# First projection of an encoder block: both modulation vectors of a quarter in one VectorE pass, and a written order for all engines

## The chip, the cores and the metric

The kernel runs on one NeuronCore of a Trainium2 chip. The metric is the device time of one execution in microseconds (us). Three runs of the kernel before took 1404.02 to 1405.08 us, median 1404.52.

## What is computed

One encoder layer over 1024 tokens of width 1024. The change touches its beginning, the modulated norm and part of the first projection:

```python
mod = jax.nn.silu(c) @ w_ada[l] + b_ada[l]
shift1, scale1, gate1, shift2, scale2, gate2 = jnp.split(mod, 6, axis=-1)

h = rms_norm(x, norm1_g[l]) * (1.0 + scale1[:, None, :]) + shift1[:, None, :]
z = h @ w_in[l]
```

`x` is 1024 x 1024, `w_ada` 1024 x 6144 and `w_in` 1024 x 2112, all float32. Two attention groups, an output projection and a mixture of experts follow; they are the same in both kernels.

## The kernel before

**Precision.** A projection is done in three matmuls per block (`mm3`, lines 68 to 71): rounded activation by rounded weight, rounded activation by the weight's remainder, remainder of the activation by the rounded weight. So a weight tile `wraw` becomes `whi` (ScalarE, line 134) and `wlo` (VectorE, line 135), and the activations become `hThi` and `hTlo`, transposed, in eight blocks of 128 rows of the width.

**First half of the first projection.** It gives 512 columns of `z` (576 to 1087) for the first four tiles of 128 tokens (`zs`, four accumulators in PSUM). The width is worked off in four quarters `i`, two blocks each. A quarter needs 256 entries of `shift1` and 256 of `scale1`, so 2 x 1 MB of `w_ada`, and 0.5 MB of `w_in`. Its steps:

1. The products: `w_ada` lies with 8 rows `k` of the width in each of 128 partitions, and `sc` holds SiLU(c) the same way. `adaacc` is the sum over `k` of row times `sc[k]`. For `shift1` (except in quarter 0, which uses TensorE, line 295) ScalarE scales the rows (line 148) and GpSimd adds them in three passes (lines 149 to 151); for `scale1` VectorE does one scaling and seven multiply-adds of 256 columns (lines 143 and 145).
2. The column sums: four matmuls of `adaacc` by ones (line 300) into `pab`.
3. VectorE: `b1` (shift), `t8`, and `a1` = (1 + scale) x gain (lines 302 to 304).
4. Per block (`flip_x`): four transposes of x tiles (line 187), `hThi` on ScalarE (line 272), the same once more unrounded as `hf` on VectorE (line 273), `hTlo` = `hf` - `hThi` (line 274).
5. 24 projection matmuls (lines 69 to 71).

The x tiles are normalised first by `norm_x` (lines 260 to 266): square with a sum, root, reciprocal, scaling.

**Second half.** The other four x tiles (`xs2`) are loaded and normalised at the end of quarter 3 (line 264 scales them on ScalarE) and go through the same blocks, with rope on the finished outputs (`rope_q`, lines 173 to 178) in between. The first matmul of this half is the one at 72.21 us in the profile. `sinb` is the sine table, scaled once (line 315).

**What sets the order.** Before, a scheduler places the instructions of this stage on the engines. The loads are issued by SP, one after the other; an issue waits for the issue eight before it to have landed, and for its buffer. The tiles `s4` (10 buffers of 512 KB) hold `w_ada`, the second x tiles and later temporaries.

```python
def split_w(tiles, src, ks, width):
    raw, hi, lo = (w[:, ks, :width] for w in tiles)
    Y.dma_start(raw, src)
    A.copy(hi, raw)
    V.tensor_sub(lo, raw, f32(hi))
```

`Y` is SP, `A` ScalarE, `V` VectorE, `G` GpSimd, `T` TensorE.

Of the kernel before, what the change touches and what calls it, by code (L numbers as in the profile page):

```python
# [9 lines left out]
F32 = mybir.dt.float32  # L10
# [10 lines left out]
D = 1024  # L21
# [30 lines left out]
def tile_hymba(  # L52
# [86 lines left out]
    def ada_sum(pool, w, eng):  # L139

        acc = pool.tile([128, 256], F32, name="adaacc", tag="adaacc")
        if eng is V:
            V.tensor_scalar(acc, w[0][:, 0], sc[:, 0:1], None, op0=ALU.mult)
            for k in range(1, 8):
                V.scalar_tensor_tensor(acc, w[k // 4][:, k % 4], sc[:, k:k + 1], acc, op0=ALU.mult, op1=ALU.add)
        else:
            for k in range(8):
                A.activation(w[k // 4][:, k % 4], w[k // 4][:, k % 4], AF.Copy, scale=sc[:, k:k + 1])
            G.tensor_add(w[0], w[0], w[1])
            G.tensor_add(w[0][:, 0:2], w[0][:, 0:2], w[0][:, 2:4])  # L150
            G.tensor_add(acc, w[0][:, 0], w[0][:, 1])
        return acc
# [73 lines left out]
    with tc.tile_pool(name="s1a", bufs=2, **RT) as sa, tc.tile_pool(name="s1r", bufs=1, **RT) as sr:  # L226
        cc = sr.tile([128, 8], F32, name="cc")
        Y.dma_start(cc, c[0].rearrange("(p k) -> p k", k=8))
        A.activation(sc, cc, AF.Silu)
        rows = sr.tile([72, 128], F32, name="rows")  # L230
# [37 lines left out]
        def flip_x(xs, j, half):  # L268
# [4 lines left out]
            V.tensor_scalar(hf, ptr, a1[:, j:j + 1], b1[:, j:j + 1], op0=ALU.mult, op1=ALU.add)  # L273
# [5 lines left out]
        adas = [ada_load(0), ada_load(4)]  # L279
        xs = [load_x(t) for t in range(4)]  # L280
        for xt in xs:
            norm_x(xt, False)
        xs2 = []
        t8 = sr.tile([128, 8], F32, name="t8")
        for i in range(4):
            qs = slice(2 * i, 2 * i + 2)
            if i:
                adas = [ada_load(i), ada_load(4 + i)]
            split_w(wq0[i // 2], wi[:, 2 * i:2 * i + 2, 576:1088], slice(2 * (i % 2), 2 * (i % 2) + 2), 512)
            pab = mps()  # L290
# [15 lines left out]
            for j in range(2 * i, 2 * i + 2):  # L306
                flip_x(xs, j, 0)
# [1325 lines left out]
```

## Time and profile before

| | |
|---|---|
| runs, median (lowest to highest) | 1404.52 us (1404.02 to 1405.08) |
| profiled execution, its own time | 1404.29 us |
| its span in the profile | 1402.5 us |
| TensorE busy over the span | 1304.8 us (93%) |
| VectorE busy | 1082.4 us (77%) |
| ScalarE busy | 771.9 us (55%) |
| GpSimd busy | 537.5 us (38%) |
| first half of the first projection, first matmul of it | 24.48 us from the span's start |
| second half, first matmul | 72.21 us |

PE is TensorE's matmul row, PEld its weight loads, DVE VectorE, ACT ScalarE, POOL GpSimd, SP the queue that issues loads. Times in the rows are from the span's start. A matmul's duration holds its way through the array, which the next one overlaps, so their pace is read from the distance of two starts. In rows of stretches the number before the DMA columns is the granted clock of TensorE as a share of 2.4 GHz.

### The profile page before, as it was taken

The numbers are of one execution on the slowest core, as the hardware profiler recorded it, in microseconds if no ns is written. First come the engines' busy times: TensorE is split into PE (matmuls) and PEld (weight loads), VectorE is DVE, ScalarE is ACT, GpSimd is POOL, SyncE is SP. The second block draws the span as 40 slices with busy tenths as digits, with TensorE's granted clock in tenths as the row PEclk, the third lists the DMA queues.
The fourth block names the chain that finished last, engine by engine and source line by source line (L and its number), as shares of the span: only waits on it lengthen the run. The fifth ranks groups of instructions, "written<-read, shape, count | busy, mean of one in ns | idle before, by whom it ended". The sixth has DMA issues, their size and how long they took to land. (4 is left out here: it accounts for less than half of the span.)

```text
span 1402.5 us, 18267 instructions
## 1 busy us (share of the span) xinstructions
PE 1304.8 (93%) x6343; PEld 1050.9 (75%) x6343; DVE 1082.4 (77%) x1610; ACT 771.9 (55%) x1194; POOL 537.5 (38%) x361
## 2 busy tenths in 40 slices
PE   5799999887999999989995999999999989999993
PEld 4578789765888888878884777777777767777762
DVE  5887646557788888874568798888888888888876
ACT  5531224346666766661224667766666756666653
POOL 2102100047666666650002244444444532544332
PEclk9899999998999999999995999999999999999995
DMA  9528963681344525238966999999989997999946
GB/s 330 163 91 265 309 234 123 182 306 53 87 139 113 172 84 192 71 132 291 342 229 256 357 367 361 356 380 372 324 318 329 354 342 286 363 375 356 380 153 246
DMA packets 123969, 357.06 MB, mean 255 GB/s; under 512 B 15781, under 2 KB 41474, under 8 KB 122338
## 3 DMA queue, kind: packets, MB, share of 16 engines
q1 hardware_dynamic: 79794, 200.11, 41.1%
q10 hardware_dynamic: 29376, 113.25, 21.2%
q0 software_dynamic: 14704, 42.51, 10.0%
q8 instruction: 51, 0.84, 0.2%
q14 instruction: 44, 0.36, 0.1%
HBM read 306.52 MB, written 57.69 MB: 260 GB/s over the span
## 5 line engine op out<-in xcount | busy, mean ns | idle before, releaser
L1176 DVE TENSOR_TENSOR ra<-rb,ra 128x1024 fp32r<-128x1024 f32 x249 | 290.5, 1220 | 51.5 <-ACT ra L1175 47.3
L1348 POOL DMA_INDIRECT x_d<-y,tg x32 | 223.4, 6983 | 124.0 <-DVE y L1418 108.5
L1175 ACT CAST ra<-rb 128x1024 fp32r<-128x1024 f32 x249 | 242.4, 1049 | 1.9 <-PE pg L70 1.3
L626 PE MATMUL s<-ra 128*128 128x512 f32 x448 | 130.8, 409 | 5.1 <-DVE stg L592 3.1
L1176 DVE TENSOR_TENSOR ra<-rx,ra 128x1024 fp32r<-128x1024 f32 x103 | 120.5, 1217 | 17.0 <-ACT ra L1175 14.6
L647 ACT ACTIVATE e<-s,mx 128x1024 f32<-128x1024 f32 x96 | 107.5, 1120 | 38.4 <-DVE mx L642 21.5
L642 DVE TENSOR_REDUCE mx<-s 128x1 f32<-128x1024 f32 x96 | 116.7, 1217 | 12.4 <-PE s L626 12.3
L69 PE MATMUL pz<-whi,hThi 128*128 128x512 f32 (+2 forms) x320 | 118.6, 371 | 5.1 <-ACT hThi L272 5.1
L70 PE MATMUL pz<-wlo,hThi 128*128 128x512 f32 (+2 forms) x320 | 116.5, 364 | 0.4 <-DVE wlo L135 0.4
L69 PE MATMUL pg<-ra,xT 128*128 128x512 f32 x256 | 114.9, 449 | 0.1
L953 POOL DMA_INDIRECT xb<-h_d,tg x31 | 31.0, 999 | 219.1 <-PE ptr L1354 198.7
L71 PE MATMUL pz<-whi,hTlo 128*128 128x512 f32 (+2 forms) x320 | 112.8, 360 | 0.1
L70 PE MATMUL pg<-ra,xT 128*128 128x512 f32 x256 | 102.3, 400 | 6.9 <-DVE ra L1176 6.9
L658 ACT CAST rb<-ptr 128x512 fp32r<-128x512 f32 x128 | 74.3, 588 | 59.8 <-PE ptr L654 59.1
L69 PE MATMUL pu<-ra,xT 128*128 128x512 f32 x256 | 104.1, 407 | 0.0
L71 PE MATMUL pg<-ra,xT 128*128 128x512 f32 x256 | 102.9, 402 | 1.1 <-DVE xT L1437 1.1
L1175 ACT CAST ra<-rx 128x1024 fp32r<-128x1024 f32 x103 | 101.2, 1048 | 2.3 <-DVE ra L1176 1.4
L70 PE MATMUL pu<-ra,xT 128*128 128x512 f32 x256 | 101.1, 395 | 0.1
L71 PE MATMUL pu<-ra,xT 128*128 128x512 f32 x256 | 101.2, 395 | 0.0
L626 PEld LDWEIGHTS s<-ra 128*128 128x128 f32 x448 | 81.6, 191 | 22.8 <-ACT e L647 4.2
L659 DVE TENSOR_TENSOR rb<-ptr,rb 128x512 fp32r<-128x512 f32 x128 | 86.3, 680 | 9.7 <-ACT rb L658 9.5
L654 PE MATMUL ptr<-ident,e 128*128 128x128 f32 x512 | 78.0, 275 | 9.0 <-POOL e L802 5.3
(365 smaller groups left out, 3020.9 us busy)
## 6 DMA issues: line engine op xcount, KB each, us to landing
rb<-in_w_expert_up_dram ACTq DMA_DIRECT2D x26, 1024.0 KB
rb<-in_w_expert_down_dram ACTq DMA_DIRECT2D x26, 1024.0 KB
rb<-in_w_expert_gate_dram ACTq DMA_DIRECT2D x24, 1024.0 KB
rb<-in_w_expert_gate_dram SPq DMA_DIRECT2D x20, 1024.0 KB
rb<-in_w_expert_down_dram SPq DMA_DIRECT2D x20, 1024.0 KB
rb<-in_w_expert_up_dram SPq DMA_DIRECT2D x19, 1024.0 KB
aw<-in_w_ada_dram SPq DMA_DIRECT2D x32, 512.0 KB
ra<-qk_d SPq DMA_DIRECT2D x48, 256.0 KB
```

The lines of the kernel that those rows point to most:

```text
L69: T.matmul(ps, ahi, bhi, start=first, stop=False)
L70: T.matmul(ps, ahi, blo, start=False, stop=False)
L71: T.matmul(ps, alo, bhi, start=False, stop=last)
L626: T.matmul(ps[:, ns], l, r[:, ns], start=i == 0, stop=i == len(parts) - 1)
L642: V.reduce_max(mx, ps, axis=AX.X, negate=True)
L647: A.activation(e, ps, AF.Exp, bias=nb, scale=1.0, accum_out=z)
L654: T.transpose(ptr[:, i * 128:(i + 1) * 128], e[:, (4 * b + i) * 128:(4 * b + i + 1) * 128], ident)
L658: A.copy(hi[:, :, q], src)
L659: return lambda: V.tensor_sub(lo[:, :, q], src, f32(hi[:, :, q]))
L1175: A.copy(hi, raw[:, 2 * half:2 * half + 2])
L1176: V.tensor_sub(lo, raw[:, 2 * half:2 * half + 2], f32(hi))
L1348: G.indirect_dma_start(out=x2_d, out_offset=bass.IndirectOffsetOnAxis(ap=si, axis=0), in_=y, in_offset=None, bounds_check=S - 1, oob_is_er ...
```

## The change

- `w_ada` is loaded so that the 256 columns of `shift1` and of `scale1` lie side by side, in eight loads of 256 KB per quarter where there were four of 512 KB. One scaling and seven multiply-adds of 512 columns on VectorE give both sums. ScalarE's and GpSimd's part in it is gone, and so is quarter 0's way over TensorE. `adaacc` has one buffer.
- The four x tiles are loaded ahead of `w_ada`, and `hf` is made on ScalarE in both halves.
- The stage is written inside `manual_schedule`, so each engine runs its instructions as they stand in the text; products for quarter `i + 1` are laid between the steps of quarter `i`. The second x tiles are normalised two in quarter 2 and two in quarter 3.
- Per block, the eight matmuls with `hThi` come first and the four with `hTlo` after them.
- A root of a constant (`sqt`) is added behind the SiLU in the text.

```diff
@@ -136,19 +136,15 @@
 
     wa = w_ada[0].rearrange("(p k) n -> p k n", k=8)
 
-    def ada_sum(pool, w, eng):
-
-        acc = pool.tile([128, 256], F32, name="adaacc", tag="adaacc")
-        if eng is V:
-            V.tensor_scalar(acc, w[0][:, 0], sc[:, 0:1], None, op0=ALU.mult)
-            for k in range(1, 8):
-                V.scalar_tensor_tensor(acc, w[k // 4][:, k % 4], sc[:, k:k + 1], acc, op0=ALU.mult, op1=ALU.add)
-        else:
-            for k in range(8):
-                A.activation(w[k // 4][:, k % 4], w[k // 4][:, k % 4], AF.Copy, scale=sc[:, k:k + 1])
-            G.tensor_add(w[0], w[0], w[1])
-            G.tensor_add(w[0][:, 0:2], w[0][:, 0:2], w[0][:, 2:4])
-            G.tensor_add(acc, w[0][:, 0], w[0][:, 1])
+    def ada_sum(pool, w):
+
+        acc = pool.tile([128, 512], F32, name="adaacc", tag="adaacc", bufs=1)
+        for k in range(8):
+            wk = w[k // 2][:, k % 2].rearrange("p v n -> p (v n)")
+            if k == 0:
+                V.tensor_scalar(acc, wk, sc[:, 0:1], None, op0=ALU.mult)
+            else:
+                V.scalar_tensor_tensor(acc, wk, sc[:, k:k + 1], acc, op0=ALU.mult, op1=ALU.add)
         return acc
 
     def in_proj(t, width, w, ps, ds=range(8)):
@@ -225,8 +221,10 @@
     sc = consts.tile([128, 8], F32, name="sc")
     with tc.tile_pool(name="s1a", bufs=2, **RT) as sa, tc.tile_pool(name="s1r", bufs=1, **RT) as sr:
         cc = sr.tile([128, 8], F32, name="cc")
+        sqt = sr.tile([128, 1], F32, name="sqt")
         Y.dma_start(cc, c[0].rearrange("(p k) -> p k", k=8))
         A.activation(sc, cc, AF.Silu)
+        A.activation(sqt, epsc, AF.Sqrt)
         rows = sr.tile([72, 128], F32, name="rows")
         V.memset(rows, 0.0)
         Y.dma_start(rows[0:48], b_ada[0].rearrange("(k p) -> k p", p=128))
@@ -250,9 +248,10 @@
             return xt
 
         def ada_load(n):
-            w = [tile_s().rearrange("p (k n) -> p k n", k=4) for _ in range(2)]
-            for h in range(2):
-                Y.dma_start(w[h], wa[:, 4 * h:4 * h + 4, n * 256:(n + 1) * 256])
+            w = [tile_s().rearrange("p (k v n) -> p k v n", k=2, v=2) for _ in range(4)]
+            for q in range(4):
+                for v in range(2):
+                    Y.dma_start(w[q][:, :, v], wa[:, 2 * q:2 * q + 2, v * D + n * 256:v * D + (n + 1) * 256])
             return w
 
         def norm_x(xt, on_act):
@@ -270,46 +269,97 @@
             ptr = flip([xt[:, j * 128:(j + 1) * 128] for xt in xs])
             hf = sa.tile([128, 512], F32, name="hf", tag="hf", bufs=2)
             A.activation(hThi[:, j, hs], ptr, AF.Identity, bias=b1[:, j:j + 1], scale=a1[:, j:j + 1])
-            V.tensor_scalar(hf, ptr, a1[:, j:j + 1], b1[:, j:j + 1], op0=ALU.mult, op1=ALU.add)
+            A.activation(hf, ptr, AF.Identity, bias=b1[:, j:j + 1], scale=a1[:, j:j + 1])
             V.tensor_sub(hTlo[:, j, hs], hf, f32(hThi[:, j, hs]))
 
 
         wq0 = [w_tiles() for _ in range(2)]
         zs = [zps() for t in range(4)]
-        adas = [ada_load(0), ada_load(4)]
         xs = [load_x(t) for t in range(4)]
-        for xt in xs:
-            norm_x(xt, False)
-        xs2 = []
+        adas, accs, xs2 = {}, {}, []
         t8 = sr.tile([128, 8], F32, name="t8")
-        for i in range(4):
-            qs = slice(2 * i, 2 * i + 2)
-            if i:
-                adas = [ada_load(i), ada_load(4 + i)]
-            split_w(wq0[i // 2], wi[:, 2 * i:2 * i + 2, 576:1088], slice(2 * (i % 2), 2 * (i % 2) + 2), 512)
+        w_part = [(wq0[i // 2], slice(2 * (i % 2), 2 * (i % 2) + 2)) for i in range(4)]
+
+        def ask(i):
+
+            if i < 4:
+                adas[i] = ada_load(i)
+                (raw, _, _), ks = w_part[i]
+                Y.dma_start(raw[:, ks], wi[:, 2 * i:2 * i + 2, 576:1088])
+
+        def prods(i, ks):
+
+            if i < 4:
+                if 0 in ks:
+                    accs[i] = sa.tile([128, 512], F32, name="adaacc", tag="adaacc", bufs=1)
+                for k in ks:
+                    wk = adas[i][k // 2][:, k % 2].rearrange("p v n -> p (v n)")
+                    if k == 0:
+                        V.tensor_scalar(accs[i], wk, sc[:, 0:1], None, op0=ALU.mult)
+                    else:
+                        V.scalar_tensor_tensor(accs[i], wk, sc[:, k:k + 1], accs[i], op0=ALU.mult, op1=ALU.add)
+
+        def part_sums(i):
             pab = mps()
...
+            for j in range(4):
+                T.matmul(pab[:, j:j + 1], accs[i][:, j * 128:(j + 1) * 128], ones[:, 0:1], start=True, stop=True)
+            return pab
+
+        def turns(i):
+            return [flip([xt[:, j * 128:(j + 1) * 128] for xt in xs]) for j in (2 * i, 2 * i + 1)]
+
+        def modulate(ptr, j):
+            hf = sa.tile([128, 512], F32, name="hf", tag="hf", bufs=2)
+            A.activation(hThi[:, j, 0:512], ptr, AF.Identity, bias=b1[:, j:j + 1], scale=a1[:, j:j + 1])
+            A.activation(hf, ptr, AF.Identity, bias=b1[:, j:j + 1], scale=a1[:, j:j + 1])
+            return hf
+
+        def proj_hi(d):
             for t in range(4):
...
+                for w in w_part[d // 2][0][1:]:
+                    T.matmul(zs[t], hThi[:, d, t * 128:(t + 1) * 128], w[:, d % 4], start=d == 0 and w is w_part[0][0][1],
+                             stop=False)
+
+        def proj_lo(d):
+            for t in range(4):
+                T.matmul(zs[t], hTlo[:, d, t * 128:(t + 1) * 128], w_part[d // 2][0][1][:, d % 4], start=False, stop=d == 7)
+
+        with tc.manual_schedule():
+            ask(0)
+            ask(1)
+            for xt in xs:
+                norm_x(xt, False)
+            prods(0, range(8))
+            ptrs, pab = turns(0), part_sums(0)
+            for i in range(4):
+                qs = slice(2 * i, 2 * i + 2)
+                ask(i + 2)
+                if i == 1:
+                    xs2 += [load_x(4 + k) for k in range(4)]
+                (raw, hi, lo), ks = w_part[i]
+                A.copy(hi[:, ks], raw[:, ks])
+                V.tensor_sub(lo[:, ks], raw[:, ks], f32(hi[:, ks]))
+                prods(i + 1, [0])
+                V.tensor_add(b1[:, qs], pab[:, 0:2], colsb[:, qs])
+                V.tensor_add(t8[:, qs], pab[:, 2:4], colsb[:, 8 + 2 * i:10 + 2 * i])
+                V.scalar_tensor_tensor(a1[:, qs], t8[:, qs], 1.0, colsb[:, 48 + 2 * i:50 + 2 * i],
+                                       op0=ALU.add, op1=ALU.mult)
+                for n in range(2):
+                    j = 2 * i + n
+                    hf = modulate(ptrs[n], j)
+                    prods(i + 1, (1 + 2 * n, 2 + 2 * n))
+                    V.tensor_sub(hTlo[:, j, 0:512], hf, f32(hThi[:, j, 0:512]))
+                    proj_hi(j)
+                    if n:
+                        if i >= 2:
+                            for xt in xs2[2 * i - 4:2 * i - 2]:
+                                norm_x(xt, True)
+                        prods(i + 1, (5, 6, 7))
+                        if i < 3:
+                            ptrs = turns(i + 1)
+                    proj_lo(j)
+                if i < 3:
+                    pab = part_sums(i + 1)
         Y.dma_start(cosb, cos_t.rearrange("(t p) d -> p t d", p=128))
         Y.dma_start(sinb[:, :, 1], sin_t.rearrange("(t p) d -> p t d", p=128))
         V.tensor_scalar(sinb[:, :, 0], sinb[:, :, 1], -1.0, None, op0=ALU.mult)
```

VectorE in quarter 2, from the first `hTlo` on (names: `hf` and `hThi` are the block's modulated copies, `st` an x tile's norm, `s4` the `w_ada` rows for quarter 3). Before:

```order
L274 TENSOR_TENSOR hTlo_104<-hf_375,hThi_103 128x512
L274 TENSOR_TENSOR hTlo_104<-hf_384,hThi_103 128x512
L135 TENSOR_TENSOR wlo_130<-wraw_128,whi_129 128x1024
L145 SCALAR_TENSOR_TENSOR adaacc_438<-s4_416,sc_105,adaacc_438 128x256
L262 RECIPROCAL st_496<-st_496 128x1
L145 SCALAR_TENSOR_TENSOR adaacc_438<-s4_416,sc_105,adaacc_438 128x256
L145 SCALAR_TENSOR_TENSOR adaacc_438<-s4_417,sc_105,adaacc_438 128x256 x4
L262 RECIPROCAL st_503<-st_503 128x1
L302 TENSOR_TENSOR b1_71<-pmi_423,colsb_69 128x2
```

Now:

```order
L351 TENSOR_TENSOR hTlo_104<-hf_381,hThi_103 128x512
L300 SCALAR_TENSOR_TENSOR adaacc_376<-s4_293,sc_105,adaacc_376 128x512
L300 SCALAR_TENSOR_TENSOR adaacc_376<-s4_294,sc_105,adaacc_376 128x512
L351 TENSOR_TENSOR hTlo_104<-hf_399,hThi_103 128x512
L261 RECIPROCAL st_413<-st_413 128x1
L261 RECIPROCAL st_418<-st_418 128x1
L300 SCALAR_TENSOR_TENSOR adaacc_376<-s4_294,sc_105,adaacc_376 128x512
L300 SCALAR_TENSOR_TENSOR adaacc_376<-s4_295,sc_105,adaacc_376 128x512 x2
L341 TENSOR_TENSOR wlo_132<-wraw_130,whi_131 128x1024
```

The products now have 512 columns and stand between the `hTlo` passes, and both reciprocals of the second x tiles stand together ahead of the last three products; before, the first stood between two products and the second behind all of them.

ScalarE over the same stretch, from the passes that make `hThi` on. Before:

```order
L272 ACTIVATE hThi_103<-ptr_370,b1_71,a1_70 128x512
L272 ACTIVATE hThi_103<-ptr_379,b1_71,a1_70 128x512
L134 CAST whi_129<-wraw_128 128x1024
L260 ACTIVATE hThi_103,st_496<-s4_494 128x2x512
L261 ACTIVATE st_496<-st_496,epsc_67 128x1
L260 ACTIVATE hThi_103,st_503<-s4_501 128x2x512
L264 ACTIVATE s4_494<-s4_494,st_496 128x1024
L261 ACTIVATE st_503<-st_503,epsc_67 128x1
L260 ACTIVATE hThi_103,st_510<-s4_508 128x2x512
```

Now:

```order
L313 ACTIVATE hThi_103<-ptr_355,b1_71,a1_70 128x512
L314 ACTIVATE hf_381<-ptr_355,b1_71,a1_70 128x512
L313 ACTIVATE hThi_103<-ptr_360,b1_71,a1_70 128x512
L314 ACTIVATE hf_399<-ptr_360,b1_71,a1_70 128x512
L259 ACTIVATE hThi_103,st_413<-s4_305 128x2x512
L260 ACTIVATE st_413<-st_413,epsc_67 128x1
L263 ACTIVATE s4_305<-s4_305,st_413 128x1024
L259 ACTIVATE hThi_103,st_418<-s4_307 128x2x512
L260 ACTIVATE st_418<-st_418,epsc_67 128x1
L263 ACTIVATE s4_307<-s4_307,st_418 128x1024
L340 CAST whi_131<-wraw_130 128x1024
```

`hf` has joined `hThi`; the weight's rounding (CAST) now stands behind both normalisations, which run square, root, scaling for one tile and then for the next.

VectorE at the end of the first half, from quarter 3's `hTlo` on (`pz` are the outputs, `st` the norms of the last two x tiles). Before:

```order
L274 TENSOR_TENSOR hTlo_104<-hf_457,hThi_103 128x512
L274 TENSOR_TENSOR hTlo_104<-hf_466,hThi_103 128x512
L262 RECIPROCAL st_510<-st_510 128x1
L262 RECIPROCAL st_517<-st_517 128x1
L173 TENSOR_TENSOR s4_526<-pz_131,cosb_101 128x512
L175 TENSOR_TENSOR s4_526<-pz_131,sinb_102 128x8x32 x2
L173 TENSOR_TENSOR s4_557<-pz_132,cosb_101 128x512
L178 TENSOR_TENSOR xt_525<-s4_526 128x512
```

Now:

```order
L351 TENSOR_TENSOR hTlo_104<-hf_450,hThi_103 128x512
L351 TENSOR_TENSOR hTlo_104<-hf_466,hThi_103 128x512
L169 TENSOR_TENSOR s4_497<-pz_133,cosb_101 128x512
L261 RECIPROCAL st_478<-st_478 128x1
L171 TENSOR_TENSOR s4_497<-pz_133,sinb_102 128x8x32 x2
L169 TENSOR_TENSOR s4_528<-pz_134,cosb_101 128x512
L174 TENSOR_TENSOR xt_496<-s4_497 128x512
L171 TENSOR_TENSOR s4_528<-pz_134,sinb_102 128x8x32 x2
L261 RECIPROCAL st_483<-st_483 128x1
```

The two reciprocals stood ahead of the rope work; now the first stands behind the first rope product and the second behind the rope work of the second output.

## Rows read from the trace of the kernel before

**Rows 1.** Busy time by stretch (start:end and length in us, then busy us and count per engine, granted clock, DMA).

```profile
5.60:70.60 65.00, 45.00 (x192) 36.52 (x193) 48.76 (x84) 37.01 (x66) 14.85 (x9) 0.92 0.78 254
72.20:99.66 27.46, 27.37 (x133) 21.40 (x133) 23.22 (x38) 8.95 (x11) 1.38 (x2) 1.00 0.24 70
```

**Rows 2.** The list of waits, 0 to 75 us (total us, times, longest us).

```profile
ACT hThi L272 <- DVE a L304: 18.8, 3, 10.4
PEld pmi L300 <- DVE adaacc L145: 10.4, 3, 6.0
```

**Rows 3.** Timeline (start, us, engine, line, tile, count, idle before): boundary to the last quarter.

```profile
62.83 0.51 PE L300 MATMUL pmi<-ones,adaacc 128*128 128x1 f32 x4
63.89 1.45 ACT L272 ACTIVATE hThi<-ptr,b,a 128x512 fp32r<-128x512 f32 x2 [1.10 <-DVE a L304]
64.72 0.50 PE L69 MATMUL pz<-whi,hThi 128*128 128x512 f32 x1 [1.39 <-ACT hThi L272]
```

**Rows 4.** Busy time by stretch, the loads (last columns: DMA share, GB/s).

```profile
0.00:10.00 10.00, 4.51 (x22) 4.54 (x22) 1.78 (x9) 1.49 (x2) 1.58 (x12) 1.00 0.71 222
10.00:35.00 25.00, 15.36 (x61) 11.43 (x60) 18.33 (x26) 16.45 (x33) 8.39 (x5) 1.00 1.07 373
35.00:50.00 15.00, 9.26 (x38) 7.69 (x39) 12.70 (x19) 5.58 (x11) 5.20 (x4) 0.77 0.94 300
```

**Rows 5.** Timeline of TensorE: the second half's first matmul.

```profile
72.21 0.50 PE L69 MATMUL pz<-whi,hThi 128*128 128x512 f32 x1 [0.76 <-ACT hThi L272]
```

**Rows 6.** Timeline of VectorE: passes of the first half.

```profile
9.25 1.52 DVE L145 SCALAR_TENSOR_TENSOR adaacc<-s,sc,adaacc 128x256 f32<-128x256 f32 x3
16.49 0.76 DVE L266 TENSOR_SCALAR xt<-xt,st 128x1024 f32<-128x1024 f32 x1
43.18 1.28 DVE L274 TENSOR_TENSOR hTlo<-hf,hThi 128x512 fp32r<-128x512 f32 x2
44.64 1.22 DVE L135 TENSOR_TENSOR wlo<-wraw,whi 128x1024 fp32r<-128x1024 f32 x1
```

**Rows 7.** Groups by form (count, busy us, mean ns, idle before): the 1024-column product.

```profile
L404 DVE SCALAR_TENSOR_TENSOR acc<-aw,sc,acc 128x1024 f32<-128x1024 f32 x28 | 35.8, 1280 | 16.2 <-DMA aw<-in_w_ada_dram 14.6 <-ACT acc L402 1.4
```

**Rows 8.** Timeline of TensorE: projection matmuls and transposes.

```profile
24.48 0.79 PE L69 MATMUL pz<-whi,hThi 128*128 128x512 f32 x1 [0.66 <-ACT hThi L272]
...
25.50 0.63 PE L69 MATMUL pz<-whi,hThi 128*128 128x512 f32 x1
25.93 0.63 PE L70 MATMUL pz<-wlo,hThi 128*128 128x512 f32 x1
...
45.59 0.64 PE L187 MATMUL ptr<-ident,xt 128*128 128x128 f32 x4
...
60.76 0.39 PE L69 MATMUL pz<-whi,hThi 128*128 128x512 f32 x1
60.99 0.40 PE L70 MATMUL pz<-wlo,hThi 128*128 128x512 f32 x1
```

**Rows 9.** Timeline of ScalarE: normalising x tiles.

```profile
13.50 1.06 ACT L260 ACTIVATE hThi<-xt 128x1024 fp32r<-128x1024 f32 x1 [10.79 <-DMA xt<-in_x_dram]
...
14.67 1.28 ACT L261 ACT_TABLE_LOAD   x1
15.96 0.29 ACT L261 ACTIVATE st<-st,epsc 128x1 f32<-128x1 f32 x1
...
59.04 1.16 ACT L264 ACTIVATE s<-s,st 128x1024 f32<-128x1024 f32 x1 [0.38 <-DVE st L262]
```

**Rows 10.** Busy time by stretch: TensorE's pause and the burst after it.

```profile
50.40:52.60 2.20, 0.00 (x0) 0.00 (x0) 2.09 (x4) 0.00 (x0) 0.85 (x2) 1.00 0.00 0
55.30:57.00 1.70, 1.70 (x6) 1.33 (x5) 1.70 (x4) 1.70 (x3) 0.00 (x0) 0.51 0.01 5
```

**Rows 11.** Timeline of VectorE: the first rope work.

```profile
68.24 0.69 DVE L173 TENSOR_TENSOR s<-pz,cosb 128x512 f32<-128x512 f32 x1 [0.68 <-PE pz L71]
...
68.85 0.74 DVE L175 TENSOR_TENSOR s<-pz,sinb 128x256 f32<-128x256 f32 x2
```

More of the change, by code (lines that the diff above doesn't have):

```diff
@@ L278, in tile_hymba @@
         zs = [zps() for t in range(4)]
-        adas = [ada_load(0), ada_load(4)]
         xs = [load_x(t) for t in range(4)]
-        for xt in xs:
-            norm_x(xt, False)
-        xs2 = []
+        adas, accs, xs2 = {}, {}, []
         t8 = sr.tile([128, 8], F32, name="t8")
-        for i in range(4):
-            qs = slice(2 * i, 2 * i + 2)
-            if i:
-                adas = [ada_load(i), ada_load(4 + i)]
-            split_w(wq0[i // 2], wi[:, 2 * i:2 * i + 2, 576:1088], slice(2 * (i % 2), 2 * (i % 2) + 2), 512)
-            pab = mps()
-            for s, w in enumerate(adas):
-                if i == 0 and s == 0:
-                    for j in range(2):
-                        for k in range(8):
-                            T.matmul(pab[:, j:j + 1], w[k // 4][:, k % 4, j * 128:(j + 1) * 128], sc[:, k:k + 1],
-                                     start=k == 0, stop=k == 7)
-                    continue
-                acc = ada_sum(sa, w, V if s else G)
-                for j in range(2):
-                    T.matmul(pab[:, 2 * s + j:2 * s + j + 1], acc[:, j * 128:(j + 1) * 128], ones[:, 0:1],
-                             start=True, stop=True)
-            V.tensor_add(b1[:, qs], pab[:, 0:2], colsb[:, qs])
-            V.tensor_add(t8[:, qs], pab[:, 2:4], colsb[:, 8 + 2 * i:10 + 2 * i])
-            V.scalar_tensor_tensor(a1[:, qs], t8[:, qs], 1.0, colsb[:, 48 + 2 * i:50 + 2 * i],
-                                   op0=ALU.add, op1=ALU.mult)
-            for j in range(2 * i, 2 * i + 2):
-                flip_x(xs, j, 0)
-            for t in range(4):
-                in_proj(t, 512, wq0, zs[t], range(2 * i, 2 * i + 2))
-            for _ in range(XL[i]):
-                xs2.append(load_x(4 + len(xs2)))
-                norm_x(xs2[-1], True)
```

## Prediction

> **What bounds the kernel now.** I read the busy time by stretch first. From 5.6 to 70.6 us, the first half of the first projection, TensorE is busy for 45.0 of 65 us; from 72.2 to 99.7 us, the second half, for 27.37 of 27.46 us [rows 1]. So only the first stretch has room. Next the list of waits says who holds TensorE there: ScalarE waits 18.8 us in three pieces for `a1`, and the four small sums on TensorE wait 10.4 us for VectorE's `adaacc` [rows 2]. The chain of one quarter is thus: products of `w_ada` rows, their sum in `adaacc`, the column sums, `b1`/`a1`, `hThi`, projection. The timeline shows its fixed part: column sums at 62.83, `hThi` at 63.89, first projection matmul at 64.72, 1.89 us: 0.51 for the sums, 0.55 for `b1`, `t8`, `a1` and the hand-over, 0.83 from ScalarE's start to TensorE's [rows 3]. Everything else in a quarter's wait is the products on VectorE, ScalarE and GpSimd. The DMA engines were no bound of their own: they moved 222 GB/s over the first 10 us and 373 GB/s to 35 us, then fell to 300 while the buffers waited for the products [rows 4]. The first half's last matmuls are followed at 72.21 by the first matmul of the second half [rows 5]. I work out when that matmul runs after the change; what follows it is bound by TensorE and should move with it.
>
> **The change, part by part.** *Prices.* The product of 512 columns is not in the trace. Before, 256 columns took 1.52/3 = 0.51 us and 1024 columns take 1.28 [rows 6, 7]; a straight line between them gives 0.76, my value, and the ends stay as bounds. The first product of a quarter is a plain scaling; 1024 columns of that take 0.76 [rows 6], so I take 0.5 for 512. `hTlo` is 1.28/2 = 0.64 and `wlo` 1.22 [rows 6]. The second modulated copy `hf` moves to ScalarE, where two passes of that kind take 1.45 [rows 3]. Four of them per quarter are 2.9 us of ScalarE. Projection matmuls start 0.23 us apart (60.76, 60.99) at full clock, but 0.43 apart (25.50, 25.93) at the start of a quarter [rows 8].
>
> *Start.* The four x tiles go ahead of `w_ada` in SP's queue. They are 2.1 MB, so by 222 GB/s the last is there at about 9.6 us, the first at about 5.2. ScalarE: square 1.06, table load 1.28, root 0.29 [rows 9], then about 1.37 per further tile (1.06 and 0.29, with gaps). The fourth root ends at 11.95 and VectorE's scaling of 0.76 at 13.0. The extra root at the top, meant to load the root's table early, comes before the Silu in the order, which loads its own table again; so the 1.28 stays where it was. VectorE has the products queued behind the fourth tile: 13.0 + 0.5 + 7 x 0.76 = 18.8. Their data (2.1 MB x, 2.1 MB `w_ada`) are there at 10 + 2.0/0.373 = 15.4, so they wait for nothing. The column sums, 0.51 [rows 3] doubled at a slow start, lie beside `wlo` (to 20.0); then the next quarter's first product, which shares the single `adaacc` buffer and must follow the column sums, 0.5; then 0.55 and 0.83 [rows 3]. First projection matmul: 21.9, against 24.48 before [rows 8].
>
> *Quarters 0 and 1.* TensorE needs 24 x 0.23 = 5.6 and 0.9 for eight transposes (four take 0.64 with their tail [rows 8]), 6.5 in all; the first eight matmuls of quarter 0 at 0.43 add 1.6 and the following ones 0.3: 30.3. The boundary is 1.89 + 0.5 for the product placed in it = 2.4: quarter 1 starts at 32.7, quarter 2 at 32.7 + 6.5 + 2.4 = 41.6. VectorE needs only 7 x 0.76 + 2 x 0.64 + 1.22 = 7.8 of those 8.9 us, ScalarE 2.9 and one rounding of a weight. GpSimd has no arithmetic left. So TensorE and the boundary set the pace here.
>
> *Quarter 2.* Here the normalisation of two x tiles of the second half is written behind the second `hTlo`: on VectorE both reciprocals stand ahead of the last three products for quarter 3. ScalarE's four passes run from 40.8 to 43.7; square with its read-out and root end at 45.25, the reciprocal at 45.45, the scaling of 1.16 [rows 9] at 46.6, the second square and root at 48.15, the second reciprocal at 48.35. Only then the three products, to 50.65. Without the reciprocals they would have ended before TensorE was through at 48.1, so this is a new wait of 2.5 us. `wlo` to 51.9; 0.55 [rows 3], the sine table's scaling that the scheduler puts in between, some 0.3, and 0.83: quarter 3 starts at 53.5.
>
> *Quarter 3.* 24 x 0.23 = 5.6. Before, TensorE did nothing from 50.4 to 52.6, and after its next burst had begun it was granted 0.51, the 1.2 GHz level, at 55.3 [rows 10]. Quarter 3 has the same pause ahead of it (48.1 to 53.5 with only the column sums inside), so I add 1.5 us (eight matmuls at 0.2 more): 60.6.
>
> *Tail.* The last two x tiles are normalised behind quarter 3. ScalarE has squared the third tile by then and rounded the next weight. VectorE reaches the third reciprocal only behind the first rope product (0.69 [rows 11]), which needs the first finished output at 60.2: 61.05. ScalarE scales (1.16) to 62.3, squares and roots the fourth tile to 63.8; VectorE's rope work (two 0.74, two of 0.69 [rows 11]) ends at 63.9; reciprocal 64.1, scaling 65.3, transposes 0.3, `hThi` 0.8: second half at 66.5. Before 72.21, so **5.7 us earlier**.
>
> *At nothing.* Weight and x loads: the tightest is the fifth x tile, wanted by ScalarE at 43.7; 13.1 MB are moved by its end, so at 10 + 10.9/0.373 = 39.2 it is there, a cover of 4 us. Each product frees its buffer at least 8 us before the load that reuses it must land. The second half's `hf` (eight passes, 5.8 us) goes to ScalarE, busy 8.95 of 27.46 there, from VectorE, busy 23.22; TensorE has 0.1 us of idle time in it [rows 1], so neither gain nor loss, and I allow 1 us each way for the new order. Later instructions stand as before but for single swaps of neighbours.
>
> *A rule against it.* The `w_ada` loads are cut from 512 to 256 KB each. The rows show 373 GB/s with several 512 KB loads under way [rows 4]. The Trainium skill, "DMA: Bandwidth & Descriptors", section Bandwidth, advises batches of at least 1 MiB and lists 138 GB/s for 64 KB and 341 for 1 MB; by it the smaller loads could carry markedly less, and the loads would become the bound. No run here shows it yet; rival 4 prices what it would do. No row shows 256 KB loads in a queue either; I go by 373 GB/s, since in both kernels eight issues may be open at once.
>
> **Sum.** The profiled execution took 1404.29 us; 1404.29 - 5.7 = 1398.6. The median of three runs is 0.23 above it, hence 1398.8.
>
> **Rivals.**
> 1. *More pays off* (0.20): the clock stays at 2.4 GHz in quarter 3 (-1.5) and a product costs nearer 0.69, as other 512-column passes do [rows 11] (ten on the path of the start and quarter 2, -0.7). 1396.6.
> 2. *Slow start of every quarter* (0.15): before, the first quarter began with matmuls 0.43 apart [rows 8], the third was granted 0.51 [rows 10], and the mean clock from 35 to 50 us, where the second lies, was 0.77 [rows 4]. Two more slow starts at 1.5: 1401.8. Against it: the last quarter of before began with a matmul of 0.50, against 0.79 in the first [rows 3, 8], after a pause of 1.39; the new boundaries pause some 2.4 with the column sums inside. [...]
> 3. *The clock stays down through all quarters* (0.04): each matmul at 0.43 costs 0.2 more. My sum holds 18 such; another 29 eat the 5.7 us, and from there it is slower. All 96 slow are 78 x 0.2 = 15.6 more: 1414.
> 4. *Loads bind* (0.05): 256 KB loads move less than 512 KB ones. The sixth x tile (13.6 MB) is wanted at 46.6, and its reciprocal stands ahead of the last three products, so quarter 3 comes later by as much as it does. This begins under 11.4/36.6 = 311 GB/s after 10 us, and under 11.4/42.3 = 270 the 5.7 us are gone. At the nearest low row, 222 [rows 4], it lands at 61.4: 14.8 later, 1413.6, slower. Against it: 373 with 1 KB runs in both kernels, and only the count of issues doubles.
> 5. *It doesn't do what it says*: true of the root's table, priced at nothing above; not of the rest, as the order shows.
>
> **Numbers.** The forecast has 0.56. A difference of 0.2%, 2.8 us, is about what can be told from none. Faster by more (below 1401.7): the forecast, rival 1 and 0.04 of rival 2, together 0.80; within it the rest of rival 2 and 0.02 of mild cases of rivals 3 and 4, 0.13; slower 0.07. The range runs from 1393.8 (rival 1 with the ten products on the path at 0.51 instead of 0.69, -1.8, and 1 us in the second half) to 1402.8 (rival 2 and 1 us); the upper bound of the product, 1.28, would make VectorE's 7.8 us into 11.4 and lies outside: the two measured ends leave little doubt about the line.
>
> **What would show it.** Right: product of 512 columns near 0.76; first projection matmuls of the quarters near 21.9, 32.7, 41.6 and 53.5; a wait of VectorE for ScalarE's root before the reciprocals at about 44 to 48; the second half's first matmul near 66.5 and 27 to 28 us of it after. Wrong: projection matmuls 0.43 apart beyond the first of a quarter; VectorE or ScalarE waiting for `w_ada`, `w_in` or x loads after 16 us; the second half longer than 28.5 us.

## The result, and the profile after

The change made the kernel **slower**: median 1411.75 us (1409.49 to 1413.30) against 1404.27 in the same series, a ratio of 1.0055 (95%: 1.0045 to 1.0066), by which it is 7.7 us more. The forecast was 5.7 us less. The profiled execution took 1413.3 us, the longest of the six and 14.7 above the 1398.6 of the sum.

I read the starts of the four quarters and of the second half first. TensorE in the changed kernel, timeline (column sums and first matmuls of the bursts):

```profile
23.12 0.79 PE L320 MATMUL pz<-whi,hThi 128*128 128x512 f32 x1 [1.79 <-ACT hThi L313]
...
34.33 0.79 PE L320 MATMUL pz<-whi,hThi 128*128 128x512 f32 x1 [1.78 <-ACT hThi L313]
...
42.38 0.95 PE L305 MATMUL pmi<-ones,adaacc 128*128 128x1 f32 x8
45.10 0.50 PE L320 MATMUL pz<-whi,hThi 128*128 128x512 f32 x1 [1.78 <-ACT hThi L313]
...
53.65 1.05 PE L305 MATMUL pmi<-ones,adaacc 128*128 128x1 f32 x8 [1.83 <-DVE adaacc L300]
56.16 0.80 PE L320 MATMUL pz<-whi,hThi 128*128 128x512 f32 x1 [1.46 <-ACT hThi L313]
...
69.88 0.79 PE L69 MATMUL pz<-whi,hThi 128*128 128x512 f32 x1 [0.66 <-ACT hThi L271]
```

The second half begins at 69.88: 2.3 us earlier than before [rows 5], where 5.7 were forecast. So the first stage fell short, but it did gain. Busy time by stretch (the columns of [rows 1]) gives a part of the reason: the granted clock was low in quarter 1, where the sum had full clock, and in quarter 3, where the sum had allowed 1.5 us for it. It was low again at the second half's start, which comes behind the 69.88.

```profile
23.10:34.30 11.20, 9.43 (x40) 7.78 (x40) 8.19 (x15) 3.83 (x6) 0.00 (x0) 1.00 1.09 366
34.30:45.10 10.80, 8.99 (x40) 7.44 (x40) 8.23 (x15) 3.75 (x6) 0.00 (x0) 0.85 1.06 365
45.10:56.10 11.00, 7.77 (x40) 6.24 (x40) 7.32 (x15) 8.63 (x14) 0.00 (x0) 0.94 0.38 106
56.10:63.80 7.70, 7.64 (x22) 6.05 (x23) 1.40 (x3) 5.04 (x8) 0.00 (x0) 0.65 0.61 155
69.90:75.00 5.10, 5.10 (x16) 4.21 (x17) 3.87 (x5) 3.16 (x5) 0.00 (x0) 0.50 0.49 129
```

The loss must lie behind. I set the same points of both traces side by side:

| TensorE's first instruction of | before | changed | difference |
|---|---|---|---|
| second half | 72.21 | 69.88 | -2.33 |
| A: the small `pmi<-ls` matmul, same 96 projection matmuls later | 99.66 | 98.78 | -0.88 |
| B: next stage, last transposes of the first four ropes | 134.64 | 134.93 | +0.29 |
| C: same stage, first transposes of the last pair | 155.10 | 159.89 | +4.79 |
| D: columns 0 to 255 | 197.70 | 203.19 | +5.49 |
| E: columns 256 to 575 | 224.76 | 233.21 | +8.45 |

After that it lies between about 8 and 9.7. The second half took 28.9 us for 27.5 before, by its start at the lower clock. The rest, over 9 us, is lost at three places behind it, between A and B, B and C, D and E. VectorE in the changed kernel, timeline, the passes ahead of which it waited at these places (and one wait that was forecast, at 51.21):

```profile
51.21 0.16 DVE L261 RECIPROCAL st<-st 128x1 f32<-128x1 f32 x1 [2.59 <-ACT st L260]
...
121.34 0.76 DVE L171 TENSOR_TENSOR rt<-pz,sinb 128x256 f32<-128x256 f32 x2 [8.21 <-DMA qk_d<-s]
...
149.01 1.28 DVE L454 SCALAR_TENSOR_TENSOR acc<-aw,sc,acc 128x1024 f32<-128x1024 f32 x1 [5.75 <-DMA aw<-in_w_ada_dram]
...
200.30 1.29 DVE L454 SCALAR_TENSOR_TENSOR acc<-aw,sc,acc 128x1024 f32<-128x1024 f32 x1 [4.49 <-DMA aw<-in_w_ada_dram]
```

and TensorE, which waits for what stands behind them:

```profile
125.21 0.55 PE L183 MATMUL ptr<-ident,rp 128*128 128x128 f32 x3 [1.10 <-DVE rp L174]
...
128.87 0.44 PE L183 MATMUL ptr<-ident,rp 128*128 128x128 f32 x2 [1.02 <-DVE rp L174]
...
153.41 0.90 PE L183 MATMUL ptr<-ident,rp 128*128 128x128 f32 x4 [2.55 <-DVE rp L174]
...
206.72 0.39 PE L70 MATMUL pz<-wlo,hThi 128*128 128x256 f32 x1 [1.83 <-DVE wlo L135]
```

The same passes in the kernel before, VectorE and then TensorE; at the second place TensorE had no wait at all:

```profile
116.28 0.69 DVE L173 TENSOR_TENSOR rt<-pz,cosb 128x512 f32<-128x512 f32 x1 [1.49 <-DMA qk_d<-s]
...
147.18 2.61 DVE L404 SCALAR_TENSOR_TENSOR acc<-aw,sc,acc 128x1024 f32<-128x1024 f32 x2 [1.66 <-DMA aw<-in_w_ada_dram]
```

```profile
148.84 0.81 PE L187 MATMUL ptr<-ident,rp 128*128 128x128 f32 x6
...
199.78 0.39 PE L70 MATMUL pz<-wlo,hThi 128*128 128x256 f32 x1 [0.39 <-DVE wlo L135]
```

`qk_d` is where the first outputs are stored, `aw` the `w_ada` rows of the four other modulation vectors (three buffers of 512 KB), `rt` and `rp` the rope temporaries and results of the next stage.

A wait costs more than its length where the clock falls behind it. The changed kernel behind its waits at 153.41 and 206.72:

```profile
153.40:157.00 3.60, 3.59 (x11) 3.01 (x12) 3.60 (x3) 0.00 (x0) 0.00 (x0) 0.54 0.77 197
206.70:212.00 5.30, 5.28 (x31) 5.28 (x32) 4.91 (x6) 2.05 (x4) 0.77 (x1) 0.68 0.92 283
```

The third wait (at 200) stands ahead of a weight remainder in both kernels, 4.49 us now; it was not taken apart by itself. TensorE's wait behind it was 0.39 us before and 0.30 in experiment 4 below, which has the old order at the new addresses; with the new order it was 1.77 to 1.84 in the five kernels at the new addresses and 0.30 to 1.81 in the five at the old ones. So it takes the new order, and the addresses have a part. The rest of the 3.0 us from D to E is the clock: experiment 8, behind a wait of 1.77 us, was granted 1.00 and lost 1.3 us there.

```profile
202.80:208.10 5.30, 5.30 (x44) 5.30 (x45) 4.91 (x7) 2.83 (x7) 0.77 (x1) 1.00 0.94 291
```

**The first is a matter of addresses.** A pool gives out its space in the order in which its tiles are first named. The change names the x tiles first, so they moved under the next stage's tiles (first byte in each partition, as the built programs have it):

```
                     before     changed
s4 (10 x 4 KB)        82048       98432
xt (4 x 4 KB)        123008       82048
aw (3 x 4 KB)         82048       82048
rt1, rt2 (4 x 2 KB)  115904      115904
```

Before, the first `aw` buffers lay on `s4` tiles and had to wait for the stores out of them; now they lie on x tiles, which come free earlier. SP's queue before, then of the changed kernel:

```profile
114.77 7.11 SPq L374 DMA_DIRECT2D aw<-in_w_ada_dram  x4
```

```profile
103.61 9.59 SPq L424 DMA_DIRECT2D aw<-in_w_ada_dram  x4
```

They go out 11 us earlier, beside the stores. Issue to landing of the stores from 85 to 130 us, before and changed:

```profile
DMA to landing us min/median/max: 2.3/3.1/6.1
```

```profile
who waited for it (us, times):
  DVE rt L171: 8.2, 1
  POOL qk_d L124: 1.5, 2
...
DMA to landing us min/median/max: 2.5/7.0/8.2
```

### The profile page after: what moved, and what is told of

Read it like the earlier page. It is cut to its first block, busy times and chain, and to the rows that moved or that the text cites. A ratio compares the mean times of both kernels' runs of the same rounds, so it can differ in the third digit from the quotient of the medians.

```text
span 1411.6 us, 18212 instructions
## 1 busy us (share of the span) xinstructions
PE 1303.8 (92%) x6315; PEld 1050.1 (74%) x6315; DVE 1068.2 (76%) x1594; ACT 776.1 (55%) x1188; POOL 522.3 (37%) x352
## 5 line engine op out<-in xcount | busy, mean ns | idle before, releaser
L69 PE MATMUL pz<-whi,hThi 128*128 128x512 f32 (+2 forms) x288 | 105.0, 365 | 0.7 <-ACT hThi L271 0.7
L70 PE MATMUL pz<-wlo,hThi 128*128 128x512 f32 (+2 forms) x288 | 103.4, 359 | 1.8 <-DVE wlo L135 1.8
L71 PE MATMUL pz<-whi,hTlo 128*128 128x512 f32 (+2 forms) x288 | 103.0, 359 | 0.0
```

The costliest lines, as they stand in the source:

```text
L69: T.matmul(ps, ahi, bhi, start=first, stop=False)
L70: T.matmul(ps, ahi, blo, start=False, stop=False)
L71: T.matmul(ps, alo, bhi, start=False, stop=last)
```

## The experiments

Ratios are to the kernel before on the same chip, whose median in these series was 1403.6 to 1403.9. The profiles, as differences to the kernel before at the points of the table above (us):

| | A | B | C | D | E |
|---|---|---|---|---|---|
| changed kernel | -0.9 | +0.3 | +4.8 | +5.5 | +8.5 |
| 1: old places | -3.4 | -4.8 | -0.5 | +0.1 | +3.1 |
| 2: changed, `hf` on VectorE | -0.5 | +0.4 | +3.7 | +4.4 | +5.9 |
| 3: 1, `hf` on VectorE | -2.9 | -4.3 | -0.1 | +0.5 | +1.3 |
| 4: before, new places | +0.2 | +4.9 | +5.0 | +5.0 | +4.8 |
| 5: old places, products behind | -0.7 | -2.2 | -2.3 | -1.3 | -0.9 |
| 8: new places, products behind | -0.4 | +0.8 | +0.8 | +1.6 | +2.9 |
| 9: new places, loads held | +0.2 | -1.3 | +1.3 | +2.0 | +3.4 |
| 6: 1 and norms on the way | -8.7 | -9.9 | -5.5 | -5.0 | -4.2 |
| 7: 5 and norms on the way | -8.7 | -10.1 | -10.2 | -9.2 | -9.3 |
| 10: 7 at the new places | -6.8 | -5.6 | -5.7 | -4.7 | -3.3 |

From A to B the new places lose 0.9 to 1.2 us with the new order (changed kernel, 2, 8, 10) and 4.6 with that of the kernel before (4); the old ones gain 1.2 to 1.5 (1, 3, 5, 6, 7). From B to C the order loses 4.5 us in the changed kernel, 4.3 in 1 and in 6, 3.2 and 4.2 in 2 and 3; in 5, 7, 8 and 10 nothing is lost there. Each row is one execution, in part the longest of its kernel, and holds its clock too; so the medians say what a change is worth, and the rows say where.

**1. Old places, new order.**

```diff
+        early = [tile_s() for _ in range(4)]
         xs = [load_x(t) for t in range(4)]
...
-            w = [tile_s().rearrange("p (k v n) -> p k v n", k=2, v=2) for _ in range(4)]
+            w = [(early.pop(0) if early else tile_s()).rearrange("p (k v n) -> p k v n", k=2, v=2) for _ in range(4)]
```

> The changed kernel with one thing undone: the first four s4 tiles are named ahead of the four x tiles, so that all tiles of the first stage lie at the addresses that they had in the kernel before; the order of every engine's instructions stays that of the changed kernel. Theory 'places' (the x tiles, now named first, have moved to the lowest addresses; the three aw buffers of the next stage now lie on x tiles and come free at 103.6 us instead of 114.8, their loads run beside the stores of the first outputs, and the rope tiles rt lie on s4 tiles whose stores are under way: VectorE's 8.2 us wait): the first aw load goes out at 111 to 115 us, VectorE's wait for a store before its first rt passes falls below 3 us, TensorE never idles over 1 us between 110 and 160 us, and the run takes 1400 to 1404 us. Rival 'order' (the scheduler laid the products of aw and the weight remainders otherwise once hf stood on ScalarE): 1409 to 1413. Rival 'time' (the second half merely starts earlier and meets the same queue at a worse moment): 1409 to 1413.

Measured: 1407.14 us (1.0022, 1.0011 to 1.0033). It gives back 4.6 us of the loss; neither theory alone. The order of every engine's instructions is that of the changed kernel in the built program, so it is the addresses that give it back. Of the signs expected of 'places', the first `aw` load came at 109.77 (said 111 to 115), VectorE's wait for a store is 5.57 us (said under 3), and TensorE still idles over 1 us. The waits on VectorE and TensorE that are left:

```profile
117.46 0.69 DVE L174 TENSOR_TENSOR rp<-rt,rt 128x512 f32<-128x512 f32 x1 [5.57 <-DMA qk_d<-s]
...
143.80 1.28 DVE L455 SCALAR_TENSOR_TENSOR acc<-aw,sc,acc 128x1024 f32<-128x1024 f32 x1 [5.64 <-DMA aw<-in_w_ada_dram]
```

```profile
148.19 0.66 PE L183 MATMUL ptr<-ident,rp 128*128 128x128 f32 x4 [2.44 <-DVE rp L174]
```

The wait for a store is shorter and TensorE no longer waits behind it; the wait for `aw` and TensorE's behind it are as in the changed kernel.

**2 and 3. `hf` of the second half back on VectorE**, at the new places and at the old ones.

```diff
-            A.activation(hf, ptr, AF.Identity, bias=b1[:, j:j + 1], scale=a1[:, j:j + 1])
+            V.tensor_scalar(hf, ptr, a1[:, j:j + 1], b1[:, j:j + 1], op0=ALU.mult, op1=ALU.add)
             V.tensor_sub(hTlo[:, j, hs], hf, f32(hThi[:, j, hs]))
```

> The changed kernel with hf of the second half back on VectorE; this also brings back the old order of the products of aw on VectorE in the next stage, while the tiles keep their new addresses. Theory 'places': 1409 to 1413 us, VectorE's wait for a store before the rt passes still over 5 us. Rival 'order': 1400 to 1405. Rival 'time': 1409 to 1413.

> Both undone: old addresses and hf of the second half on VectorE with the old order of the next stage. What is left of the change is the first half alone. Places and order: 1400 to 1404 us (the second half starts 2.3 us earlier than in the kernel before and nothing is lost behind it). Rival 'time': 1408 to 1413. If places and order each carry a part, this one is the fastest of the first three by over 1.5 us.

Measured: 1409.93 (1.0039, 1.0027 to 1.0052) and 1406.77 (1.0025, 1.0016 to 1.0034). One thing in both expectations was wrong: the order of the `aw` products did not come back with `hf`; the built programs keep that of the changed kernel. So these two test `hf` alone: by the medians 1.8 and 0.4 us less than without it, by the ratios 2.2 less and 0.4 more, with intervals that overlap. They say nothing on the order, and what in the change made the scheduler lay the products otherwise stays open.

**4. The kernel before, at the new places.**

```diff
+        early = [tile_x() for _ in range(4)]
+
         def load_x(t):
-            xt = tile_x() if t < 4 else tile_s()
+            xt = early[t] if t < 4 else tile_s()
```

> The kernel before with nothing changed but the addresses: its four x tiles are named ahead of the s4 tiles; the order on every engine is that of the kernel before. Theory 'places': slower than before by 5 to 10 us (1409 to 1414), first aw load near 104 to 107 us, a wait of VectorE for a store before the rt passes of 5 to 10 us. Rivals 'order' and 'time': 1403 to 1405.5, as before.

Measured: 1408.40 us (1.0033, 1.0021 to 1.0045): 4.5 us for the addresses alone, a little under the range, and against both rivals. The order of every engine is that of the kernel before in the built program. The first `aw` load went out at 106.53, and VectorE shows the wait, TensorE two waits behind it:

```profile
124.03 0.69 DVE L173 TENSOR_TENSOR rt<-pz,cosb 128x512 f32<-128x512 f32 x1 [8.98 <-DMA qk_d<-s]
```

```profile
126.72 0.41 PE L187 MATMUL ptr<-ident,rp 128*128 128x128 f32 x2 [1.62 <-DVE rp L178]
128.49 0.69 PE L187 MATMUL ptr<-ident,rp 128*128 128x128 f32 x2 [1.36 <-DVE rp L178]
```

The two are 3.0 of the 4.6 us between A and B; behind them TensorE began at the lower clock (0.68 granted from 126.7 to 130.0).

**5 and 8. The order of the products**, at the old and at the new places. VectorE around the last two tiles' ropes, before and changed (from the built programs, by tiles):

```
before                                      changed
rt_1155<-pz,cosb   rt_1156<-pz,sinb x2      acc<-aw,sc,acc
rp<-rt_1155,rt_1156                         rt_1126<-pz,cosb   rt_1127<-pz,sinb x2
acc<-aw,sc,acc  x2                          acc<-aw,sc,acc
wlo<-wraw,whi 128x2048                      rp<-rt_1126,rt_1127
rt_1190<-pz,cosb   ...                      acc<-aw,sc,acc
                                            wlo<-wraw,whi 128x2048
```

One tile's rope stood ahead of the first product shown; in the changed kernel that rope stands behind it, and it is the product that waits 5.75 us at 149.01. The edit queues the later stage's products behind the eighth rope, so it is not the order of the kernel before but one with no such product ahead of a rope:

```diff
-                rope(sb, pz.rearrange("p (m h d) -> p m h d", m=8, h=2), 8, t, rp)
+                last = rope(sb, pz.rearrange("p (m h d) -> p m h d", m=8, h=2), 8, t, rp)
...
-            ada_add(AC[t])
+            with tc.issue_after(last.ins):
+                ada_add(AC[t])
```

> Old places as in the first experiment, and on VectorE the products of aw that belong to the stage after the next queue behind the last rope of the next stage (before, two of them stood ahead of the seventh tile's rope only as a whole behind the sixth; in the changed kernel one stands ahead of it and waits 5.6 us for its aw load, TensorE then idles 2.4 us at 148 us and goes on at 0.43 us a matmul). Theory 'order': that order costs 3 to 4 us, so TensorE has no idle time over 1 us between 140 and 160 us and the run takes 1402 to 1404.5 us. Rival 'loads' (the aw loads set the pace whatever the order; the lead is lost a little later, at the weight remainder near 201 us or at the norms near 234): 1406 to 1408, with a longer wait of TensorE at 195 to 240 us.

> The changed kernel at its own places, with the products alone moved behind the last rope. Theory: places and order add up, so 3 to 4 us less than the changed kernel: 1407 to 1409, with the 8 us wait of VectorE for a store near 121 us still there and no wait of TensorE at 153. Rival 'loads': 1410 to 1412.

Measured: 1404.78 (1.0001, 0.9992 to 1.0010) at the old places, 1408.00 (1.0028, 1.0017 to 1.0039) at the new: 2.4 and 3.7 us less than without the edit (2.9 and 3.8 by the ratios), the first 0.3 above its range. TensorE from 146 to 156 us, stretch of experiment 1, then of experiment 5:

```profile
146.00:156.00 10.00, 6.48 (x30) 5.04 (x31) 10.00 (x13) 1.67 (x3) 0.17 (x1) 1.00 0.77 217
```

```profile
146.00:156.00 10.00, 10.00 (x53) 8.32 (x52) 8.64 (x10) 3.90 (x5) 1.97 (x4) 1.00 0.64 177
```

The idle time is gone, as the theory 'order' said; small waits of TensorE, 0.83 and 1.03 us at 199 and 230, are what the rival got right. Experiment 8 kept its 8.3 us wait for a store at 121.92 and has no wait at 153. Places and order together are 7.0 us by the medians and 7.6 by the ratios, nearly all of the loss. In the built program of experiment 5 two `w_in` loads also go out three `aw` loads earlier than in experiment 1, so what it gains behind C is not the products' place alone. And with both losses undone the change is worth nothing that can be told from noise (1.0001); a gain came only with the next edit.

**6 and 7. The norms on the way**, without and with the edit of experiment 5, old places.

```diff
                         if i >= 2:
-                            for xt in xs2[2 * i - 4:2 * i - 2]:
-                                norm_x(xt, True)
+                            sts += [root_x(xt) for xt in xs2[2 * i - 4:2 * i - 2]]
+                        if i == 3:
+                            for xt, st in zip(xs2, sts):
+                                tail_v = scale_x(xt, st)
...
-            rope_q(zs[i], i, rps[i])
+            with tc.issue_after(tail_v.ins):
+                rope_q(zs[i], i, rps[i])
...
-                in_w(1088, 512, 1)
+                with tc.issue_after(tail_v.ins), tc.issue_after(st_a[-1].ins):
+                    in_w(1088, 512, 1)
```

`root_x` is the square and the root of `norm_x`, `scale_x` its reciprocal and scaling, on VectorE.

> Old places, and the four second x tiles are normalised on the way: ScalarE only squares and roots them in quarters 2 and 3, VectorE takes the reciprocals and the scalings behind quarter 3's hTlo, all ahead of the rope work; so no reciprocal stands ahead of quarter 3's products any more. Expected by the step of the tail: the second half's first matmul at 61 to 64 us (69.9 in the changed kernel), at full clock. Theory 'order': most of it is lost again at 140 to 160 us behind the aw loads: 1404 to 1407. If the early stage sets the time after all: 1399 to 1402.

> Both of the last two edits on the old places. Theory 'order': the 6 to 8 us of an earlier second half are kept through the next stage: 1396 to 1400. Rival 'loads': 1402 to 1407, TensorE's waits are found at 195 to 240 us.

Measured: 1398.08 (0.9952, 0.9939 to 0.9965) and **1397.41** (0.9948, 0.9936 to 0.9961), 7.3 us under the kernel before by the ratio and 6.3 by the medians: the last is the best version found. In it TensorE starts the second half with

```profile
63.36 0.47 PE L69 MATMUL pz<-whi,hThi 128*128 128x512 f32 x1 [0.81 <-DVE s L171]
```

and the first 5 us are at full clock:

```profile
63.30:68.50 5.20, 4.46 (x23) 3.38 (x24) 5.02 (x10) 4.65 (x7) 0.00 (x0) 1.00 0.00 0
```

Experiment 7 came as the theory 'order' said, experiment 6 did not: I had expected most of the earlier start to be lost behind the `aw` loads, and it was not. Its trace still has TensorE's wait,

```profile
143.09 0.66 PE L183 MATMUL ptr<-ident,rp 128*128 128x128 f32 x4 [2.35 <-DVE rp L174]
```

and loses 4.3 us from B to C, but the execution profiled, of 1400.59 us, was the longest of its five, and the medians of 6 and 7 lie only 0.7 us apart, with overlapping intervals. What the order of the products is worth once the second half begins early is left open.

**9. The early loads held back**, new places and new order.

```diff
             aw[i] = ap.tile([128, D], F32, name="aw", tag="aw", bufs=AB)
+            if i < AB:
+                tc.keep_in_program_order(G.memset(aw[i][:, 0:1], 0.0))
```

> The changed kernel at its own places and with its own order; the only addition are three clearings of one column of the aw buffers on GpSimd, which stand behind the last store of the first outputs, so that the first three aw loads cannot go out before about 115 us (103.6 to 111 in the changed kernel). It splits the effect of the places in two. Theory 'collision' (the early aw loads take the transfer engines from the stores): stores land in 3 to 5 us instead of 7.3, VectorE's wait for a store near 121 us falls from 8.2 to under 4 us, and 2 to 4 us come back: 1407.5 to 1410. Rival 'lying' (the rope tiles simply lie on s4 tiles that are stored last, whatever else is under way): the wait stays over 6 us and the run takes 1411 to 1413, or more, since the aw products are now later as well.

Measured: 1407.21 us (1.0022, 1.0012 to 1.0031), 4.5 less than the changed kernel, as much as the old places give. Loads, stores and VectorE's wait in it:

```profile
114.55 10.38 SPq L426 DMA_DIRECT2D aw<-in_w_ada_dram  x5
```

```profile
DMA to landing us min/median/max: 2.3/3.1/5.2
```

```profile
119.23 0.76 DVE L171 TENSOR_TENSOR rt<-pz,sinb 128x256 f32<-128x256 f32 x2 [5.06 <-DMA qk_d<-s]
```

So the collision is shown: with the loads 11 us later the stores land in 3.1 us again, TensorE no longer waits near 125, and from A to B 1.4 us are gained instead of 1.2 lost. Another 1.9 us came at the second place, from B to C, where the product waited 3.95 us instead of 5.75 and TensorE 0.70 instead of 2.55; I had not foreseen this, and why it is so is not shown. What is left of VectorE's wait (5.06, where I had said under 4) is again put down to a store by the profile, as the rival 'lying' has it: the rope tiles lie on tiles that are being stored. TensorE does not feel it.

**10. Experiment 7 at the new places.**

> The two edits of the seventh experiment (norms on the way, products behind the ropes) at the new places of the changed kernel. If the places cost the same wherever the second half begins: 3 to 5 us over the seventh experiment, 1400.5 to 1402.5. If the cost of the places came only from the late second half: 1397 to 1398.5.

Measured: 1400.41 us (0.9973, 0.9963 to 0.9984), 3.0 over experiment 7. By the medians the places cost 3.0 to 4.6 us in all four pairs (changed and 1, 4 and before, 8 and 5, 10 and 7), wherever the second half begins (3.5 to 4.6 by the ratios); in each pair the two intervals do not overlap. In the profiles the part from A to B is 2.6 to 2.7 us in three of the pairs and 4.6 in that of the kernel before. In the pairs changed and 1, 10 and 7, another 2.5 and 2.0 us lie ahead of A, where the executions profiled had different clocks (last section), so the 4.6 of the first pair may hold some luck.

## Why the prediction was wrong

**The step that failed** is the sentence that what follows the second half's first matmul "is bound by TensorE and should move with it", with "Later instructions stand as before but for single swaps of neighbours", both priced at nothing. The second half took 28.9 us, beyond the 28.5 that I had named as the limit, since it began at the lower clock (0.50 granted to 75.0); the stages behind it lost far more. I looked at the order and not at the addresses; the swaps were not harmless either, since the product that moved ahead of a rope waits for a load, and TensorE waits for the rope. Shown by experiments 1, 4, 8, 9 and 10 (places: 3.0 to 4.6 us) and 5, 8 (order: 2.4 and 3.7 us).

**The first stage, by its steps.** *Prices:* right. Two 512-column products took 1.53 us, so 0.77 for 0.76; a lone `hTlo` 0.69 for 0.64.

```profile
44.10 1.53 DVE L300 SCALAR_TENSOR_TENSOR adaacc<-s,sc,adaacc 128x512 f32<-128x512 f32 x2
```

*Start:* 23.12 for 21.9, and the boundary 2.7 us (42.38 to 45.10) for 2.4. The first x tile at "about 5.2" does not follow from 222 GB/s, by which its 0.5 MB takes 2.4 us, but it came true: ScalarE began at 5.02. The term mis-sized is the column sums. I took the 0.51 of [rows 3] for all four columns; they were four records, and four columns are eight, 0.95 us. *Quarter 0:* 11.2 us for 10.8. *Quarter 1:* 10.8 us for 8.9, mostly its slow first matmuls, which I had put into rival 2. *Quarter 2:* 11.1 for 11.9; the new wait for the reciprocals was there: VectorE waited 2.59 us ahead of the second one, and TensorE 1.83 us for the column sums (at 53.65), where the sum had 2.5. *Quarter 3 and tail:* 13.7 for 13.0. Together 69.88 for 66.5. That `hf` moved for neither gain nor loss holds within what experiments 2 and 3 can tell.

**The rivals.** *Slow starts* came in part, and cost quarter 1 most of its 1.9 us: the mean granted clock of quarters 1 and 3 was 0.85 and 0.65 and that of the second half's start 0.50, the 1.2 GHz level, but quarter 2 began with a matmul of 0.50 us instead of 0.79. The Trainium skill, "TensorE: Matmul & The Clock Gate", section "HAM oscillation", tells of a kernel in which every burst began at the lower level, behind waits longer than the pauses here. In this trace, behind shorter ones, quarters 1 and 3 began low and quarter 2 did not. *Loads bind* did not come: 366 GB/s in quarter 0, mostly in 256 KB loads. Going against the advice of the Trainium skill, "DMA: Bandwidth & Descriptors", section Bandwidth, to load in batches of at least 1 MiB cost nothing here by that row; its table is of loads issued from GpSimd, these are issued from SP. One sign of being wrong did come, without a cost: ScalarE waited for a `w_in` load after 16 us,

```profile
18.27 1.05 ACT L340 CAST whi<-wraw 128x1024 fp32r<-128x1024 f32 x1 [5.75 <-DMA wraw<-in_w_in_dram]
```

but `wlo`, which needs it, stands on VectorE behind the products, which ended at 19.4. *The root's table* was loaded again, as said:

```profile
2.08 0.20 ACT L227 ACTIVATE sqt<-epsc 128x1 f32<-128x1 f32 x1
2.31 1.28 ACT L226 ACT_TABLE_LOAD   x1
6.18 1.28 ACT L260 ACT_TABLE_LOAD   x1
```

None of the rivals had the stage behind; those on the slower side, 3 and 4, looked for the loss in the first projection.

## What to carry to other kernels

Which tile is named first decides what lies under the next pool's tiles, and with it when the next stage's loads may start: after a rewrite compare the addresses, not only the order. Rerun the old order at the new addresses and the new order at the old ones: it separates the two in two runs. And a load that may start earlier is not a gain in itself: ask which stores it meets, and who waits for the space under them.

## What had not been expected of the hardware

Four loads of 512 KB beside the stores took the stores' median from issue to landing from 3.1 to 7.0 us, and holding them back brought 3.1 again. And one and the same order of instructions got different clocks. Up to quarter 2's first matmul the order is the same in the changed kernel and in all experiments but 4, and the idle time ahead of it is 1.78 us in each, behind the same column sums. Yet that matmul took 0.50 us in the changed kernel and in 2, 5, 6 and 8, and 0.73 to 0.80 in 1, 3, 7, 9 and 10. Experiment 1:

```profile
45.33 0.79 PE L321 MATMUL pz<-whi,hThi 128*128 128x512 f32 x1 [1.78 <-ACT hThi L314]
```

Its quarter 2 thus ended later, TensorE waited only 0.44 us for the next column sums instead of 1.83, and its quarter 3 was granted the full clock, where the changed kernel had 0.65:

```profile
56.30:63.00 6.70, 6.30 (x28) 4.93 (x28) 2.81 (x7) 5.69 (x9) 0.00 (x0) 1.00 0.70 178
```

Its second half began at 67.66, 2.2 us earlier. In experiment 7 it was quarter 2 that began low (0.57 from 45.6 to 49.0) and quarter 3 that did not (1.00 from 55.8 to 60.0). So behind the same idle time a burst began at either level, from one execution to the next, and no rule for it is shown here; a forecast can give such a start a chance, and one profiled execution does not settle it.
